# Softmax over rows: loads and stores of 8, 8 and seven times 16 rows, and broadcast multiplications on VectorE

## The chip, the cores and the metric

One core of a Trainium2 chip. The metric is the device time of one execution in microseconds (us), taken over several executions; all runs that are compared here are fast unless the text says otherwise. The profile is one of these executions. Its span, counted from the first load's issue to the last instruction, is about 2 us shorter than the device time.

## The reference

```python
x: (16, 1024, 512) float32
x_max = np.max(x, axis=-1, keepdims=True)
exp_x = np.exp(x - x_max)
return (exp_x / np.sum(exp_x, axis=-1, keepdims=True)).astype(np.float32)
```

That is 16384 rows of 512 numbers, 33.55 MB in and as much out.

## The kernel before

The rows are cut into chunks; a chunk of R rows per partition is one load. SBUF, the core's on-chip memory, is used in 128 partitions (the 128 in every shape below). The kernel keeps 96 rows per partition there, so the last two chunks go into rows that earlier ones have left. Within a chunk the work goes in groups of up to 8 rows per partition: VectorE takes the maxima (one instruction), ScalarE does exp and the sum row by row, VectorE the reciprocal, and GpSimd multiplies the group by it; for the last three groups VectorE multiplies. Loads are issued from SyncE, stores from ScalarE. Emission order is maximum and exponentials of group g, then scaling and store of group g-1.

```python
CHUNKS = [   # rows per partition, first row in SBUF
    (3, 0), (5, 3), (8, 8), (16, 16), (16, 32), (16, 48), (16, 64), (16, 80), (16, 0), (16, 16),
]
EARLY = 8                          # loads issued at once
AFTER_STORE = {2: [8], 3: [9]}     # chunk 8 is loaded after the store of chunk 2, 9 after 3
FINISH_BEFORE = (1, 2, 3)          # scale the waiting group before these chunks start
STORE_ROWS = {3: 8, 4: 8, 5: 8}    # chunks 3, 4, 5 are stored in halves of 8 rows
ON_VECTOR = 3
...
    def scale(g):
        k, a, b, since = groups[g]
        recip = stats.tile([P, b - a], F32, name="recip", tag="recip")
        nc.vector.reciprocal(out=recip, in_=sums[g])
        on_pool = g < len(groups) - ON_VECTOR
        if on_pool:
            nc.gpsimd.tensor_tensor(
                out=place[k][:, a:b, :], in0=place[k][:, a:b, :],
                in1=recip.unsqueeze(2).to_broadcast([P, b - a, d]),
                op=mybir.AluOpType.mult,
            )
        for r in () if on_pool else range(a, b):
            nc.vector.tensor_scalar_mul(
                out=place[k][:, r, :], in0=place[k][:, r, :],
                scalar1=recip[:, r - a : r - a + 1],
            )
        if since is not None:
            nc.scalar.dma_start(out=dst[k][:, since:b, :], in_=place[k][:, since:b, :])
        if b == CHUNKS[k][0]:
            for later in AFTER_STORE.get(k, ()):
                load(later)

        # in the order of the program
        for g, (k, a, _, _) in enumerate(groups):
            if waiting is not None and a == 0 and k in FINISH_BEFORE:
                scale(waiting)
                waiting = None
            rowmax(g)
            exps(g)
            if waiting is not None:
                scale(waiting)
            waiting = g
        scale(waiting)
```

(In this excerpt some lines are joined and comments are added.)

## Time and profile before

161.5 us. The DMA engines are full from the first microsecond to the last; the compute engines are about half busy.

| | before |
|---|---|
| device time, median of 6 | 161.51 us |
| span of the profile | 159.6 us |
| busy: VectorE, ScalarE, GpSimd | 82.6, 92.9, 91.2 us |
| DMA queues' share of 16 engines: loads, stores | 49.6%, 49.0% |
| last load landed | 109.1 us |
| last store issued | 134.0 us |
| first and last data packet | 1.0 us, 158.6 us |

### The profile page before, as it was taken

Reading aid. Unit: us, or ns where it says so; the run is one execution under the profiler, and the core shown is the slowest. Engines: PE = TensorE matmul, PEld = TensorE weight load, DVE = VectorE, ACT = ScalarE, POOL = GpSimd, SP = SyncE. Lnnn points to the kernel's source line nnn. Section 1 sums busy time; section 2 is a strip of 40 time slices with the busy share of each in tenths; the row PEclk is TensorE's granted clock in tenths of the full one; section 3 lists DMA queues with packets and bytes.
Section 4 is the critical chain, followed back from the end, with each engine's and each line's share of the span. In section 5 each row is a group of like instructions: output and inputs, shape, how many; then the busy total and the mean of one; then the engine's idle time right before and its main releaser. Section 6 shows DMA issues by size and latency. Waiting matters only on the chain.

```text
span 159.6 us, 442 instructions
## 1 busy us (share of the span) xinstructions
DVE 82.6 (52%) x58; ACT 92.9 (58%) x257; POOL 91.2 (57%) x18
## 2 busy tenths in 40 slices
DVE  0470903980966567393856768386479935000000
ACT  0719076039949796976979957993995760000000
POOL 0060912950899999999999999999930000000000
DMA  7999999999999999999999999989999999999994
GB/s 271 439 464 398 431 391 435 458 408 421 431 423 431 427 415 443 411 468 423 431 456 411 437 423 431 464 378 448 406 468 443 445 411 419 476 411 419 468 419 172
DMA packets 3315, 67.13 MB, mean 421 GB/s; under 512 B 368, under 2 KB 368, under 8 KB 624
## 3 DMA queue, kind: packets, MB, share of 16 engines
q1 hardware_dynamic: 1440, 33.56, 49.6%
q10 hardware_dynamic: 1872, 33.56, 49.0%
q14 instruction: 3, 0.02, 0.0%
HBM read 33.55 MB, written 33.55 MB: 420 GB/s over the span
## 4 chain that ended last, share of the span: by engine, by line
POOL 51%; issue 12%; ACT 11%; DVE 7%; DMA 3%; ACTq 0%; DVEq 0%; POOLq 0%
POOL held L150 51%; ACT held L135 11%; DVE held L157 4%; DMA held<-in_x_dram 3%; DVE shift L127 3%; ACTq L163 0%; DVE recip L147 0%; DVEq L209 0%; POOLq L150 0%; DVEq L147 0%; ACTq L135 0%
## 5 line engine op out<-in xcount | busy, mean ns | idle before, releaser
L135 ACT ACTIVATE held<-held,shift 128x512 f32<-128x512 f32 x128 | 90.4, 708 | 33.0 <-POOL held L150 29.9
L150 POOL TENSOR_TENSOR held<-held,recip 128x4096 f32<-128x4096 f32 (+2 forms) x14 | 91.0, 6529 | 25.8 <-DVE recip L147 25.8
L127 DVE TENSOR_REDUCE shift<-held 128x8 f32<-128x4096 f32 (+2 forms) x17 | 70.3, 4139 | 5.4 <-DMA held<-in_x_dram 5.4
L147 DVE RECIPROCAL recip<-sums 128x8 f32<-128x8 f32 (+2 forms) x17 | 3.4, 200 | 45.9 <-ACT held L135 45.9
L135 ACT ACTIVATION_READ_ACCUMULATOR held<-held,shift 128x1 f32 x128 | 24.0, 187 | 0.0
L157 DVE TENSOR_SCALAR held<-held,recip 128x512 f32<-128x512 f32 x24 | 10.0, 491 | 0.1
L135 ACT ACT_TABLE_LOAD x1 | 1.3, 1283 | 4.5 <-DMA held<-in_x_dram 4.5
L198 POOL MEMSET const-float32-0.0<- 128x1 f32 x1 | 0.1, 98 | 0.2 <-issue 0.2
L198 POOL MEMSET const-bfloat16-1.0<- 128x1 bf16 x1 | 0.1, 101 | 0.0
L198 POOL MEMSET const-uint8-127<- 128x1 uint8 x1 | 0.1, 101 | 0.0
L198 POOL MEMSET const-float32-1.0<- 128x1 f32 x1 | 0.1, 98 | 0.0
## 6 DMA issues: line engine op xcount, KB each, us to landing
held<-in_x_dram SPq DMA_DIRECT2D x7, 4096.0 KB, 39.1
out_dram<-held ACTq DMA_DIRECT2D x4, 4096.0 KB, 29.1
out_dram<-held ACTq DMA_DIRECT2D x7, 2048.0 KB, 37.9
held<-in_x_dram SPq DMA_DIRECT2D x1, 2048.0 KB, 11.5
held<-in_x_dram SPq DMA_DIRECT2D x1, 1280.0 KB, 7.1
out_dram<-held ACTq DMA_DIRECT2D x1, 1280.0 KB, 20.5
held<-in_x_dram SPq DMA_DIRECT2D x1, 768.0 KB, 4.4
out_dram<-held ACTq DMA_DIRECT2D x1, 768.0 KB, 15.8
```

The lines of the kernel that those rows point to most:

```text
L127: nc.vector.reduce_max(out=shift[g], in_=place[k][:, a:b, :], axis=AX, negate=True)
L135: nc.scalar.activation(out=place[k][:, r, :], in_=place[k][:, r, :], func=EXP, bias=shift[g][:, r - a : r - a + 1], scale=1.0, accum_out=s ...
L147: nc.vector.reciprocal(out=recip, in_=sums[g])
L150: nc.gpsimd.tensor_tensor(out=place[k][:, a:b, :], in0=place[k][:, a:b, :], in1=recip.unsqueeze(2).to_broadcast([P, b - a, d]), op=mybir.A ...
L157: nc.vector.tensor_scalar_mul(out=place[k][:, r, :], in0=place[k][:, r, :], scalar1=recip[:, r - a : r - a + 1],)
L198: nc = _bacc.Bacc("TRN2", target_bir_lowering=False, num_devices=1)
```

## The change

Its intent: fewer and larger transfers, and one instruction in place of eight for a scaling on VectorE. The diff, cut to its core (the old scaling is shown in the kernel above):

```diff
 CHUNKS = [
-    (3, 0), (5, 3), (8, 8), (16, 16), (16, 32), (16, 48), (16, 64), (16, 80), (16, 0), (16, 16),
+    (8, 0), (8, 8), (16, 16), (16, 32), (16, 48), (16, 64), (16, 80), (16, 0), (16, 16),
 ]
-EARLY = 8
-AFTER_STORE = {2: [8], 3: [9]}
+EARLY = 7
+AFTER_STORE = {1: [7], 2: [8]}
-FINISH_BEFORE = (1, 2, 3)
-STORE_ROWS = {3: 8, 4: 8, 5: 8}
+FINISH_BEFORE = ()
+STORE_ROWS = {}
@@ scale(g)
-        on_pool = g < len(groups) - ON_VECTOR
-        if on_pool:
-            nc.gpsimd.tensor_tensor(... broadcast of recip ...)
-        for r in () if on_pool else range(a, b):
-            nc.vector.tensor_scalar_mul(... row r ...)
+        engine = nc.gpsimd if g < len(groups) - ON_VECTOR else nc.vector
+        engine.tensor_tensor(
+            out=place[k][:, a:b, :],
+            in0=place[k][:, a:b, :],
+            in1=recip.unsqueeze(2).to_broadcast([P, b - a, d]),
+            op=mybir.AluOpType.mult,
+        )
```

More of the change, by code (lines that the diff above doesn't have):

```diff
@@ L147, in scale @@
         nc.vector.reciprocal(out=recip, in_=sums[g])
-        on_pool = g < len(groups) - ON_VECTOR
-        if on_pool:
-            nc.gpsimd.tensor_tensor(
-                out=place[k][:, a:b, :],
-                in0=place[k][:, a:b, :],
-                in1=recip.unsqueeze(2).to_broadcast([P, b - a, d]),
-                op=mybir.AluOpType.mult,
-            )
-        for r in () if on_pool else range(a, b):
-            nc.vector.tensor_scalar_mul(
-                out=place[k][:, r, :],
-                in0=place[k][:, r, :],
-                scalar1=recip[:, r - a : r - a + 1],
-            )
+        engine = nc.gpsimd if g < len(groups) - ON_VECTOR else nc.vector
[5 more added lines that the diff above has]
+        )
         if since is not None:
```

## The prediction

> **What bounds the kernel now.** I read the page first. The engines are 52 to 58% busy, so none of them is the limit. The DMA row and the queues are:
>
> ```profile
> DMA  7999999999999999999999999989999999999994
> DMA packets 3315, 67.13 MB, mean 421 GB/s; under 512 B 368, under 2 KB 368, under 8 KB 624
> q1 hardware_dynamic: 1440, 33.56, 49.6%
> q10 hardware_dynamic: 1872, 33.56, 49.0%
> ```
>
> The two queues (q1 loads, q10 stores) fill 98.6% of the sixteen engines' time between them. Only the first slice (until the first data) and the last (the final landing) have gaps. So the kernel is as long as 67 MB of traffic plus about 2.3 us of start and end (1.4% of 159.6 us). The page's chain of work names POOL with 51%, but that chain ends with the last scaling on VectorE at 134 us, and the span ends at 159.6. I therefore looked at the last stretches:
>
> ```profile
> core 0: us, DVE busy (x) ACT busy (x) POOL busy (x), PEclk, DMA share, GB/s
> ...
> 100.00:120.00 20.00, 12.57 (x13) 17.44 (x51) 17.21 (x3) 1.00 1.00 431
> 120.00:140.00 20.00, 11.42 (x20) 7.79 (x22) 0.00 (x0) 1.00 1.02 440
> 140.00:160.00 20.00, 0.00 (x0) 0.00 (x0) 0.00 (x0) 1.00 0.87 374
> ```
>
> No engine works after 134 us, and the DMA engines are still full. The last store was issued at 134.0 us; the queue then still had 24.6 us of packets (they end at 158.6), of which the last store itself is 8 x 1.213 = 9.7 us. So the last computation could have come about 15 us later before it cost anything. That slack is what the change can spend.
>
> How the two queues share is the second thing to read. A packet here is one partition's run: 32 KB for a load of 16 rows, 16 KB for a store of 8. Each transfer gives each engine eight packets. In the stretch from 60 to 70 us:
>
> ```profile
> q1 hardware_dynamic: 108, 3.01, 69.8%
> q10 hardware_dynamic: 103, 1.43, 33.3%
> ```
>
> Equal packets, not equal bytes: the queues alternate one for one, so a 32 KB load packet is followed by one 16 KB store packet and loads get two thirds. The trace has 1.213 us for a 32 KB packet and 0.611 for a 16 KB one; 8 x (1.213 + 0.611) = 14.6 us per load, and the last six loads land at 36.8, 50.9, 65.5, 80.0, 94.6 and 109.1 us, 14.1 to 14.6 apart. The tail after the last landing, on VectorE, is:
>
> ```profile
> 109.21 4.42 DVE L127 TENSOR_REDUCE shift<-held 128x8 f32<-128x4096 f32 x1 [0.81 <-DMA held<-in_x_dram]
> ...
> 116.75 3.52 DVE L157 TENSOR_SCALAR held<-held,recip 128x512 f32<-128x512 f32 x8
> 120.19 4.41 DVE L127 TENSOR_REDUCE shift<-held 128x8 f32<-128x4096 f32 x1
> ...
> 124.74 3.25 DVE L157 TENSOR_SCALAR held<-held,recip 128x512 f32<-128x512 f32 x8
> 130.48 0.20 DVE L147 RECIPROCAL recip<-sums 128x8 f32<-128x8 f32 x1 [2.48 <-ACT held L135]
> 130.72 3.26 DVE L157 TENSOR_SCALAR held<-held,recip 128x512 f32<-128x512 f32 x8
> ```
>
> The maximum of the last group stands behind the scaling of an earlier group, so 24.9 us pass from the landing of the last load to the issue of the last store.
>
> [...]
>
> **The change, part by part.** The bytes stay the same. The first two loads (3 and 5 rows) become one of 8, and it lands when the second did, about 7.4 us; the next 8 rows again at 12.4.
>
> Stores become 16 rows in three places where they were two halves of 8, so their packets grow from 16 to 32 KB. Per byte this is 0.6065 against 0.611 us for 16 KB: the 48 packets of 16 KB per engine that merge into 24 of 32 KB save about 0.2 us. Five DMAs fewer (18 instead of 23) save their semaphore packets of 9 ns, nothing.
>
> The first store comes later. First maximum 7.4 to 11.8, eight exponentials and the accumulator 5.8, to 17.6, reciprocal and hand-over 0.3, GpSimd 7.0: the first store is issued at 24.9 instead of 11.5 us. DMA stays busy meanwhile, with loads. In the trace the first store packet ran 3.7 us after the issue (11.5 to 15.2), because load packets lay ahead; so the first now runs at about 28.5.
>
> The sharing changes most. The third load (16 rows) lands at 12.4 + 8 x 1.27 = 22.6 (load packets with nothing beside them took 1.27 to 1.28 early on). At 28.5 five packets of the fourth are done. Left are 3 + 5 x 8 = 43 load packets on each engine, and each is paired with a store packet: 16 of 16 KB (the first two stores), then 27 of 32 KB. The last load therefore ends after 43 x 1.213 + 16 x 0.611 + 27 x 1.213 = 94.7 us, plus some 0.5 for the slower early ones: 123.7, landing at 124.1 instead of 109.1. This needs the store queue never to run dry: stores are issued, by the chain of 7.0 us scalings, at about 25, 34, 48, 62, 77 and 96 us, and needed at 28.5, 43, 58, 77, 97 and 116. It holds. The buffers for the last two loads come free at 58 and 78, before their turn.
>
> The tail from that landing, in the order in which the changed program puts VectorE's work: maximum 4.4, reciprocal and hand-over 0.4, tensor multiplication of the group before 4.4, maximum 4.4, exponentials 5.8 (the second multiplication, 4.4, lies beside them), reciprocal 0.3, multiplication 4.4: 24.1 us. The broadcast multiplications cost about 0.9 to 1.2 us each more than eight scalar ones (4.42 against 3.25 to 3.5); two of the three lie on this path. GpSimd's last scaling ends near 123, before VectorE's first at 129[...]. The last store is issued at 124.1 + 24.1 = 148.2 instead of 134.0.
>
> What is left for DMA at 123.7: 72 store packets less 43, that is 29, of which 21 lie before the last store: 21 x 1.213 = 25.5, to 149.2. An issue to an idle queue showed its first packet after 1.0 us (the first load), so the last store begins at about 149.3 to 149.7. The 15 us of slack is spent almost exactly; a gap of 0 to 0.5 us may open. Then 9.7 us of packets, the skew between engines included in the 25.5 only in part (up to 0.5), and 1.0 from last packet to end as before (158.6 to 159.6): span 160.0 to 160.9. The measured time was 1.9 above the span (161.45 against 159.6), which gives 161.9 to 162.8. I choose 162.1, since the larger packets give back 0.2.
>
> **The rivals.** First: pure traffic. If the loads end some us earlier, the last store still finds work before it, and the time is 161.2 to 161.6. For it speaks that 98.6% of the span is traffic that does not change; against it, that the pairing puts the last landing 15 us later. Second: the tail becomes the bound. Each us by which the last load lands later than 124, or by which the tail is longer than 24, then adds a whole us. If the broadcast multiplication ran at half the assumed rate on VectorE (8.8 us), the path would be 8.8 us longer and the time near 170. For that speaks only that no broadcast on VectorE is in this trace; on GpSimd the same form has no odd cost between widths (2.75 us for 1536, 7.02 for 4096 elements). Third: the late first store lets GpSimd be the bound. It starts at 17.9 instead of 8.7, but 13 equal scalings of 7.0 are 91 us, to 109 without waits and some 123 with waits for the slower loads; stores stay ahead of DMA throughout, so it costs nothing. Fourth: faster, by fewer and larger transfers. At most the 2.3 us of start and end plus 0.3 of packets could go, 1.6%, and the start is latency that stays.
>
> **Range and chances.** The two bounds, traffic at 161.3 and the tail at about 162.3, lie within 1 us of each other, and the time is the later. Errors of 1 to 2 us in the landing push it up and none pushes it below the traffic, so the range is lopsided: 161.2 to 163.5. Faster than 2% would need 158.3, below the traffic: 0.01. Slower than 2% is 164.7, a tail 2.5 us later than worked out: 0.06.
>
> **What the profile would show.** Right: equal packet counts and now about equal bytes of the two queues in the middle; the last load landing near 124; the last store issued near 148; VectorE's three multiplications of 4.4 us; DMA share near full to the end, with at most a small dent near 149. Wrong: stores not getting half of the bytes, a last landing before 120 (then 161.4) or after 127 (then 164 or more), multiplications on VectorE well off 4.4 us, or a hole in the DMA row in the middle, which would mean that the store queue ran dry.

The sum stands with all its terms: 124.1 for the last landing, 24.1 of tail, so the last store's issue at 148.2; that store's packets from 149.3 to 149.7 on, a span of 160.0 to 160.9, and with 1.9 outside it 161.9 to 162.8, of which the author chose 162.1. The terms of 4.4 us for a multiplication of 128x4096 by a broadcast on VectorE stand in it without their derivation, and the 4.42 set against the scalar ones had not been measured then. In the trace of the kernel before, the maximum over the same 128x4096 took 4.39 us in the mean, and eight multiplications by a scalar 3.25 to 3.52; the changed kernel's broadcast multiplications then took 4.42 to 4.43.

## The result, and the profile after

162.18 us, median of 6 runs (161.95 to 162.24), against 161.51 (161.40 to 161.61). The ratio is 1.0039, 95% interval 1.0026 to 1.0052. Ratios here are the mean time of one kernel's fast runs over that of the other's of the same rounds, so they are not quite the ratio of the medians. That is the same within 2%, and slower by 0.7 us beyond the noise.

The page of the changed kernel, DMA row and queues:

```profile
DMA  7999999899999999999999999999999999999996
...
q1 hardware_dynamic: 1296, 33.56, 49.6%
q10 hardware_dynamic: 1296, 33.56, 48.7%
```

Now both queues have 1296 packets, and DMA is still full, but for a dent near 149 us that the slices above are too coarse to show. In the middle, from 80 to 100 us (each line: queue, packets, MB, share of the 16 engines), the changed kernel has

```profile
q1 hardware_dynamic: 156, 4.59, 53.2%
q10 hardware_dynamic: 145, 4.23, 49.0%
```

where the kernel before had

```profile
q1 hardware_dynamic: 196, 5.90, 68.4%
q10 hardware_dynamic: 199, 2.74, 32.0%
```

In both, the two queues have packets in near equal number (196 to 199 before, 156 to 145 now), but the stores' packets have doubled in size (from 16 to 32 KB), so loads fall from 5.90 to 4.59 MB in the same 20 us. The loads are slowed by the stores (e6 below shows it with the stores alone changed), and the last one lands late. The tail in order of time (start, duration, engine and operation, and in brackets the idle time before it and what ended it):

```profile
124.00 4.42 DVE L127 TENSOR_REDUCE shift<-held 128x8 f32<-128x4096 f32 x1 [8.87 <-DMA held<-in_x_dram]
...
128.57 4.42 DVE L149 TENSOR_TENSOR held<-held,recip 128x4096 f32<-128x4096 f32 x1
...
132.91 4.41 DVE L127 TENSOR_REDUCE shift<-held 128x8 f32<-128x4096 f32 x1
...
137.47 4.43 DVE L149 TENSOR_TENSOR held<-held,recip 128x4096 f32<-128x4096 f32 x1
...
143.21 0.20 DVE L147 RECIPROCAL recip<-sums 128x8 f32<-128x8 f32 x1 [1.32 <-ACT held L135]
143.44 4.42 DVE L149 TENSOR_TENSOR held<-held,recip 128x4096 f32<-128x4096 f32 x1
147.96 0.34 ACTq L156 DMA_DIRECT2D out_dram<-held  x1
```

The last load is there at 124.0 (before: 109.1), and the last store is issued at 147.96 (before: 134.0). By stretches near that point:

```profile
core 0: us, DVE busy (x) ACT busy (x) POOL busy (x), PEclk, DMA share, GB/s
140.00:147.50 7.50, 6.15 (x3) 3.11 (x10) 0.00 (x0) 1.00 0.99 428
147.50:150.00 2.50, 0.37 (x1) 0.00 (x0) 0.00 (x0) 1.00 0.55 236
```

The kernel before has 433 GB/s in the same 2.5 us. So the queue did run dry for a moment: summed over the trace's packets, each engine idles 0.64 us on average in this stretch. The trace also shows why this costs less than 0.64: the sixteen engines end the packets of the second-last store between 147.9 and 149.2 us, and the last store's first packets run from 148.8. The engines that were early wait; the slowest one (149.2) does not, and its 149.2 plus 9.7 us for its eight packets of the last store gives 158.9, which is where the last packet ended (158.86). Before, the last packets of the engines ended 1.07 us apart; now, after the common restart, 0.3 apart.

The head is the other place with a difference. The first stretches of the kernel before, and then of the changed one:

```profile
0.00:2.00 2.00, 0.00 (x0) 0.00 (x0) 0.20 (x4) 1.00 0.48 135
2.00:4.00 2.00, 0.00 (x0) 0.00 (x0) 0.00 (x0) 1.00 0.99 407
```

```profile
0.00:2.00 2.00, 0.00 (x0) 0.00 (x0) 0.20 (x4) 1.00 0.73 131
2.00:4.00 2.00, 0.00 (x0) 0.00 (x0) 0.00 (x0) 1.00 0.87 336
```

From 2 to 4 us the changed kernel moves 336 GB/s against 407. The first packet of each engine took 1.00 to 2.23 us for 16 KB, where later ones take 0.61; before, 0.23 to 0.64 us for 6 KB, where later ones take 0.234. The first 16 rows had landed at 13.0 instead of 12.4 us.

So two theories stand for the 0.7 us. The **tail theory**: the last store comes too late. The **head theory**: the first loads start slower. The experiments undo one or the other.

### The profile page after: what moved, and what is told of

It is laid out like the page before. It is cut to its first block, busy times and chain, and to the rows that moved or that the text cites. A ratio compares the mean times of both kernels' runs of the same rounds, so it can differ in the third digit from the quotient of the medians.

```text
span 160.0 us, 405 instructions
## 1 busy us (share of the span) xinstructions
DVE 85.8 (54%) x35; ACT 92.9 (58%) x257; POOL 91.1 (57%) x17
## 3 DMA queue, kind: packets, MB, share of 16 engines
q1 hardware_dynamic: 1296, 33.56, 49.6%
q10 hardware_dynamic: 1296, 33.56, 48.7%
## 4 chain that ended last, share of the span: by engine, by line
DMA 52%; POOL 17%; issue 11%; DVE 9%; ACT 4%; DVEq 0%; POOLq 0%; SPq 0%
DMA held<-in_x_dram 33%; DMA out_dram<-held 20%; POOL held L149 17%; DVE held L149 6%; ACT held L135 4%; DVE shift L127 3%; DVE recip L147 0%; POOLq L149 0%; SPq L122 0%; DVEq L147 0%; DVEq L149 0%; DVEq L127 0%
## 5 line engine op out<-in xcount | busy, mean ns | idle before, releaser
L149 POOL TENSOR_TENSOR held<-held,recip 128x4096 f32<-128x4096 f32 x13 | 90.9, 7018 | 31.9 <-DVE recip L147 31.9
L127 DVE TENSOR_REDUCE shift<-held 128x8 f32<-128x4096 f32 x16 | 70.4, 4400 | 49.8 <-DMA held<-in_x_dram 49.8
L149 DVE TENSOR_TENSOR held<-held,recip 128x4096 f32<-128x4096 f32 x3 | 13.3, 4425 | 0.1
L147 DVE RECIPROCAL recip<-sums 128x8 f32<-128x8 f32 x16 | 3.2, 199 | 12.2 <-ACT held L135 12.2
```

The costliest lines, as they stand in the source:

```text
L127: nc.vector.reduce_max(out=shift[g], in_=place[k][:, a:b, :], axis=AX, negate=True)
L149: engine.tensor_tensor(out=place[k][:, a:b, :], in0=place[k][:, a:b, :], in1=recip.unsqueeze(2).to_broadcast([P, b - a, d]), op=mybir.AluO ...
```

## The experiments

Eleven kernels were run, and all gave correct results. "Outside" is device time less span, mean over the fast runs.

| run | time, us (median) | ratio to before, 95% interval | mean span | outside |
|---|---|---|---|---|
| changed kernel | 162.18 | 1.0039 (1.0026 to 1.0052) | 160.2 | 1.97 |
| e1 changed, small first loads | 162.32 | 1.0050 (1.0037 to 1.0062) | 160.1 | 2.23 |
| e2 changed, half stores | 162.26 | 1.0044 (1.0031 to 1.0056) | 160.2 | 2.04 |
| e3 changed, scalar multiplications | 161.86 | 1.0018 (1.0005 to 1.0032) | 160.1 | 1.83 |
| e6 before, whole stores only | 161.74 | 1.0016 (1.0004 to 1.0029) | 160.0 | 1.81 |
| e4 changed, 4.4 us more tail | 166.23 | 1.0295 (1.0281 to 1.0308) | 164.2 | 2.07 |
| e5 before, 4.4 us more tail | 161.59 | 1.0008 (0.9995 to 1.0021) | 159.8 | 1.84 |
| e7 changed, 16 rows first | 169.4 (its two fast runs; 171.1 with the two slow ones) | none | 167.5 | 1.89 |
| e8 before, 1 row first | 162.06 | 1.0042 (1.0027 to 1.0057) | 160.3 | 1.81 |
| e9 changed, padded program | 161.86 | 1.0028 (1.0014 to 1.0041) | 160.2 | 1.81 |
| e10 before, broadcasts only | 161.67 | 1.0018 (1.0002 to 1.0034) | 159.8 | 2.01 |
| e11 before, first loads only | 161.98 | 1.0030 (1.0017 to 1.0043) | 160.2 | 1.83 |

The kernel before, run beside them, had medians of 161.47 to 161.54 us, spans of 159.5 to 159.8 and 1.77 to 1.88 us outside.

### Is the slack of the tail spent? e4 and e5

The same edit in both kernels, one more multiplication (by ones) before the last store (the tile of ones and its filling are left out here):

```diff
+        if g == len(groups) - 1:
+            nc.vector.tensor_tensor(
+                out=place[k][:, a:b, :], in0=place[k][:, a:b, :],
+                in1=ones.unsqueeze(2).to_broadcast([P, b - a, d]),
+                op=mybir.AluOpType.mult,
+            )
         if since is not None:
```

> The changed kernel with one more multiplication of 128x4096 (by ones, the result is unchanged) on VectorE just before the last store: 4.4 us of extra tail. If the slack is nearly spent, as predicted (the last store is issued at 147.96 and the slowest engine has packets to 149.2, so about 0.4 us is left): a hole of 4 to 5 us in the DMA row and 166.0 to 166.6 us. If the tail does not bound the changed kernel and there is still slack: under 163 us.

> The kernel before with the same extra multiplication of 4.4 us before the last store. There the last store has some 15 us of other packets before it: 161.4 to 161.8 us, no hole. If the tail is on the path of the kernel before, as its chain of work says: 166 us.

166.23 us and 161.59. Of 4.4 us of added tail the changed kernel pays 4.05 (166.23 less 162.18) and the kernel before 0.1 (less 161.47, its neighbours' median). The stretches of the changed kernel with the longer tail:

```profile
147.50:150.00 2.50, 2.47 (x2) 0.00 (x0) 0.00 (x0) 1.00 0.06 26
150.00:152.50 2.50, 2.35 (x1) 0.00 (x0) 0.00 (x0) 1.00 0.00 0
```

and of the kernel before with it:

```profile
147.50:150.00 2.50, 0.00 (x0) 0.00 (x0) 0.00 (x0) 1.00 1.03 446
```

This is the clearest result: the changed kernel has about 0.4 us of slack left (4.43 less 4.05), the kernel before at least the 4.4 us that were added. Its whole slack is worked out, not tested: 148.9 (its slowest engine takes up the last store) less 134.0 is 14.9 us, or some 14 if the 0.84 us from the issue to the first packet (147.96 to 148.80 in the changed kernel) is counted. It also shows that the chain of work on the page of the kernel before, which ran through the tail, did not name what bounded it.

### Does the tail or the head cost the 0.7 us? e1, e2, e3, e6

e1, on the changed kernel:

```diff
-    (8, 0), (8, 8), (16, 16), ...
+    (3, 0), (5, 3), (8, 8), (16, 16), ...
-EARLY = 7
-AFTER_STORE = {1: [7], 2: [8]}
-FINISH_BEFORE = ()
+EARLY = 8
+AFTER_STORE = {2: [8], 3: [9]}
+FINISH_BEFORE = (1, 2, 3)
```

> The changed kernel with the kernel before's first loads (3, 5 and 8 rows instead of 8 and 8); whole stores and broadcast multiplications stay. The first 16 rows should land at 12.4 us again instead of 13.0. Head theory (the loss of the change lies in the slow first load alone): 161.5 us. Tail theory (the last store's issue is the bound, with almost no slack): stores start 14 us earlier, so 53 instead of 43 load packets per engine are paired with store packets; the last load lands near 125.8 instead of 124.0, and with 24 us of tail the last store is issued near 149.8: 163.2 to 163.8 us.

162.32 us: neither number. The first 16 rows landed at 12.4 as expected, but the last load landed at 124.0, not 125.8, and the last store was issued at 147.98; the pairing argument had overlooked that the store queue is empty for some 4 us before the first whole store (the last 16 KB store packets end at 53.9 us, the first of 32 KB start at 58.1), and loads run unpaired meanwhile: up to the end of the loads each engine took 50.8 store packets, not 53. DMA idles 0.86 us on average per engine from 147.5 to 150, and the span is 160.1.

e2, on the changed kernel:

```diff
-STORE_ROWS = {}
+STORE_ROWS = {2: 8, 3: 8, 4: 8}
```

> The changed kernel with chunks 2, 3 and 4 stored in halves of 8 rows, as before. Loads get two thirds of the bytes again, the last one lands near 108, and the last store is issued some 14 us before the queue is empty. Head theory: 162.1 to 162.4 us, the loss stays (smaller packets may add 0.2). Tail theory: the loss goes, 161.5 us.

162.26 us, as the head theory has it. The last load lands at 108.0, the last store is issued at 135.6, and the hole is gone (first the maximum that waits for the last load, then the stretch that held the hole):

```profile
108.03 4.42 DVE L127 TENSOR_REDUCE shift<-held 128x8 f32<-128x4096 f32 x1 [0.47 <-DMA held<-in_x_dram]
...
147.50:150.00 2.50, 0.00 (x0) 0.00 (x0) 0.00 (x0) 1.00 0.97 419
```

The loss stays. So taking away the hole alone doesn't bring the time back; and e1 shows that taking away the new head alone doesn't either.

e3, on the changed kernel (the diff of `scale` reversed):

```diff
-        engine = nc.gpsimd if g < len(groups) - ON_VECTOR else nc.vector
-        engine.tensor_tensor(... broadcast of recip ...)
+        ... GpSimd as before; on VectorE eight tensor_scalar_mul, as before
```

> The changed kernel with VectorE's three multiplications as eight by a scalar each, as before. The last landing stays at 124.0 and the last store is issued about 2 us earlier, near 146. Head theory: 162.1 us. Tail theory: 161.5 to 161.8 us.

161.86 us (161.67 to 162.19): between the two, 0.24 under the head theory's number and 0.06 over the tail theory's range. The store was issued at 145.8, with no hole. The spans (mean 160.1) are those of the changed kernel within noise; what fell is the time outside the span, from 1.97 to 1.83. That was not in either theory.

e6, on the kernel before:

```diff
-STORE_ROWS = {3: 8, 4: 8, 5: 8}
+STORE_ROWS = {}
```

> The kernel before with the halved stores merged into 16 rows and nothing else changed. The last load should land near 125.8 instead of 109.1, and the last store be issued near 147.7, the scalar multiplications keeping the tail at 22 us. Both theories, where the tail has a slack of about 2 us: 161.3 to 161.6 us; the difference from the small-head run is then VectorE's multiplications alone. If whole stores cost something by themselves (other than by the tail), it shows here as over 162.

161.74 us, 0.2 slower than before, a little above the range for "no cost" and below the 162 that was to show a cost of its own. The last load lands at 124.0 here too, and the last store is issued at 145.6: the whole stores alone move the last landing by 15 us, and no hole opens as long as the tail is short. e1 differs from e6 in VectorE's multiplications alone: 0.58 us, of which 0.42 is outside the span (2.23 against 1.81). Inside it, the hole of 0.86 us costs about 0.1.

### The first packet: e11, e7, e8

e11 is the head alone, on the kernel before:

```diff
-    (3, 0), (5, 3), (8, 8), (16, 16), ...
+    (8, 0), (8, 8), (16, 16), ...
-EARLY = 8
-AFTER_STORE = {2: [8], 3: [9]}
-FINISH_BEFORE = (1, 2, 3)
-STORE_ROWS = {3: 8, 4: 8, 5: 8}
+EARLY = 7
+AFTER_STORE = {1: [7], 2: [8]}
+FINISH_BEFORE = ()
+STORE_ROWS = {2: 8, 3: 8, 4: 8}
```

> The kernel before with the first two loads (3 and 5 rows) made one of 8, halved stores and scalar multiplications kept. Head theory: the first 16 rows land at 12.8 to 13.0 instead of 12.4, the span grows to 160.0 to 160.3, and the time is 161.85 to 162.1 us. If the first loads do not matter: 161.4 to 161.6.

161.98 us and spans of 160.0 to 160.3: 0.44 us over the kernel before, two thirds of what the whole change costs. In the profiled run, the fastest of the five, the first 16 rows landed at 12.6, and the first packets again took 0.69 to 1.61 us for 16 KB.

The slow first packets aren't the whole of it. Counted over the trace's packets, e11 had moved fewer bytes than the kernel before, by 0.45 us' worth (at 432 GB/s) at 14 us, but only by 0.08 at 20 us and by 0.10 to 0.11 from 60 us on: most of the slow start was won back, at the time when the kernel before begins with its first stores (15.2 us; in e11 28.8). The rest of the 0.40 us of span lies at the end: the slowest engine ends 0.88 us after the mean of the sixteen (before 0.73), and the span ends 1.18 us after the last packet (before 1.04). So "the head" is here the first loads with all that follows from them.

e7 and e8 were to show whether the size of the first packet is the cause. e7, on the changed kernel:

```diff
-    (8, 0), (8, 8), (16, 16), (16, 32), (16, 48), (16, 64), (16, 80), (16, 0), (16, 16),
+    (16, 0), (16, 16), (16, 32), (16, 48), (16, 64), (8, 80), (8, 88), (16, 0), (16, 16),
-AFTER_STORE = {1: [7], 2: [8]}
+AFTER_STORE = {0: [7], 1: [8]}
```

> The changed kernel with loads of 16, 16, 16, 16, 16, 8, 8, 16, 16 rows: the first packets are of 32 KB, and the stores are of 16 rows from the first on. Pairing: the first store starts near 41.5 us; the 40 load packets left on each engine are paired with 40 store packets of 32 KB; the last load lands near 129.7, the last store is issued near 153.7, the DMA row has a hole of about 5 us, 167 us (166 to 168). First-packet theory: the first 16 rows land at 13.3 to 14 us, later than with 16 KB packets (13.0) and with 6 KB (12.4); if it is not the packet's size, at 12.4 to 13.0.

e8, on the kernel before:

```diff
-    (3, 0), (5, 3), (8, 8), ...
+    (1, 0), (2, 1), (5, 3), (8, 8), ...
-EARLY = 8
-AFTER_STORE = {2: [8], 3: [9]}
-FINISH_BEFORE = (1, 2, 3)
-STORE_ROWS = {3: 8, 4: 8, 5: 8}
-AT_HEAD = {mybir.EngineType.SP: 3}
+EARLY = 9
+AFTER_STORE = {3: [9], 4: [10]}
+FINISH_BEFORE = (1, 2, 3, 4)
+STORE_ROWS = {4: 8, 5: 8, 6: 8}
+AT_HEAD = {mybir.EngineType.SP: 4}
```

> The kernel before with the first load of 3 rows split into 1 and 2. First-packet theory: first packets of 2 KB, the first 16 rows land at 12.0 to 12.3 us instead of 12.4, and the time is 161.2 to 161.6 us; the tail keeps its slack. If more and smaller transfers cost more than the first packet saves: 161.7 or more.

Both miss. The first maximum of e7, which waits for its first 16 rows:

```profile
12.23 4.42 DVE L127 TENSOR_REDUCE shift<-held 128x8 f32<-128x4096 f32 x1 [12.23 <-DMA held<-in_x_dram]
```

12.2 us, not 13.3 to 14, although each first packet of 32 KB took 1.5 to 2.25 us instead of 1.21. And e8, with first packets of 2 KB at their ordinary 0.08 to 0.2 us, had its first 16 rows only at 14.1: later packets were slow instead, and one engine fell 1.6 us behind the first. (This profile is of the slowest of its six runs, 162.59; but the fastest, 161.77, is over all runs of the kernel before too.) The landing of the first 16 rows against the number of loads that bring them is 12.2 (one), 12.6 to 13.0 (two of 8), 12.4 (three), 14.1 (four). There is no order by size in this, so "a larger first packet costs more in the end" is not supported. What remains is that the first packets are slow with 8 rows (0.69 to 2.23 us for 16 KB in the profiles of e11 and the changed kernel, where later ones take 0.61) and that this head alone costs 0.44 us.

e7's time (169.88 and 168.90 in its fast runs; the other two were slow) is above the 166 to 168 expected: the last load landed at 132.0, not 129.7, with the engines up to 4.4 us apart. From there the arithmetic of the tail holds: 24.0 us to the store's issue at 156.03, the first packet at 156.9, the last one's end at 166.8.

### The time outside the span: e9 and e10

The table shows 1.81 to 1.84 us outside the span for every kernel with scalar multiplications, and 1.89 to 2.23 with broadcasts. The trace has a third 8 KB fetch of instructions, at 120 to 139 us in the former. In e1, e2 and e4 it comes at 161.7, 161.9 and 166.1, after the span's end; in the changed kernel and e7 none is recorded. The broadcast makes VectorE's program 21 instructions shorter.

e9, on the changed kernel (the tile `spare`, which nothing reads, is left out here):

```diff
+            if g == 4:
+                for _ in range(21):
+                    nc.vector.memset(spare, 0.0)
             rowmax(g)
             exps(g)
```

> The changed kernel with 21 tiny VectorE instructions (128x8 memsets of a tile that nothing reads) put in before the fifth group, so that VectorE's program is about as long as that of the kernel before. In the runs so far the time outside the span is 1.80 to 1.87 us where VectorE's scalings are eight scalar instructions, and 1.91 to 2.27 where they are one broadcast; in the first kind the trace has a third 8 KB instruction fetch between 120 and 140 us, in some of the second kind it comes only after the end of the span. Fetch theory: the third fetch falls inside the span, the time outside it goes to 1.80 to 1.87, and the total to about 162.0. If the length of the program has nothing to do with it: 1.95 or more outside the span, 162.1 to 162.2 in all.

e10, on the kernel before (the diff of `scale` alone):

```diff
-        ... on VectorE eight tensor_scalar_mul
+        engine = nc.gpsimd if g < len(groups) - ON_VECTOR else nc.vector
+        engine.tensor_tensor(... broadcast of recip ...)
```

> The kernel before with VectorE's 24 scalar multiplications replaced by three broadcast ones, nothing else. The tail gets about 3 us longer and has 15 us of slack: the span stays at 159.6 to 159.8. Fetch theory: 1.95 to 2.25 us outside the span, 161.65 to 162.0 in all. If the fetch theory is wrong: 161.4 to 161.6.

Both came out as the fetch theory has it. The queue of instruction fetches on the page of e10, which has two within its span (the third is at 161.7):

```profile
q14 instruction: 2, 0.02, 0.0%
```

and of e9, where padding brought the third back, at 128.8 us:

```profile
q14 instruction: 3, 0.02, 0.0%
```

e9 has 1.81 us outside its span, as the kernel before has, and 161.86 in all (161.71 to 162.42; its spans scatter more, 159.9 to 160.6). e10 has 2.01 and 161.67. Its profiled run, 162.57, was the one outlier of six. So the length of VectorE's program, and not the broadcast as such, makes the difference. Whether the late fetch itself costs the time is not shown apart from that, nor why it is 0.42 us in e1 against e6 and 0.13 to 0.21 elsewhere.

### All eight combinations

Taken together, the runs hold every combination of the change's three parts (the new head with its order of scaling, whole stores, broadcasts). Median us, and in brackets the mean span:

| | half stores, scalar | half stores, broadcast | whole stores, scalar | whole stores, broadcast |
|---|---|---|---|---|
| first loads 3, 5, 8 | before: 161.51 (159.7) | e10: 161.67 (159.8) | e6: 161.74 (160.0) | e1: 162.32 (160.1) |
| first loads 8, 8 | e11: 161.98 (160.2) | e2: 162.26 (160.2) | e3: 161.86 (160.1) | changed: 162.18 (160.2) |

The head costs 0.4 to 0.6 us with half stores, but 0.1 and -0.1 with whole ones; whole stores cost 0.2 and 0.65 with the old head, and about -0.1 with the new one. So the two don't add up: by the ratios to the kernel before, both together cost 0.5 us (give or take 0.3, an estimate from the table's intervals) less than the sum of each alone. For the kernels with broadcasts the traces say why the head doesn't matter there: the last store's first packet runs at 148.8 in e1 as in the changed kernel, because in both the last load lands at 124.0 and the same tail follows. Here the tail is the bound; without the hole (e2) the last packet ends no sooner, at 158.89 us against 158.86. For the scalar ones the reason is open.

No experiment beat the kernel before.

## Why the prediction was right

The time was within 0.1 us of 162.1. The pairing and the tail were right; that the sum came so close was luck in part, for small errors at its start and end didn't enter or nearly cancelled.

**Traffic bounds both kernels: held.** DMA is full throughout in both (the two queues fill 98.6% of the sixteen engines' span before, 98.3% after), but for the hole in the changed one.

**The pairing of packets and the last landing: held.** 156 load packets to 145 store packets from 80 to 100 us, and the landing at 124.0 against 124.1 predicted. The kernel with whole stores alone (e6) moved the landing by the same 15 us, and half stores (e2) moved it back to 108.0.

**The tail: held.** 24.0 us from landing to issue against 24.1, multiplications of 4.42 to 4.43 us where the sum had 4.4, the issue at 147.96 against 148.2, the packets of the second-last store to 149.2. e4 shows that 0.4 us of slack is left. Of the 15 us, e5 tested 4.4, and e6 moved the issue by 11.6 us without a hole. GpSimd's last scaling had ended, at 123.2 us, before VectorE's first multiplication began, at 128.6, as said. Where the two met, the multiplication took longer: in e10 VectorE's first one starts 0.46 us before GpSimd's last one ends, and took 4.75 us; the other two took 4.42.

**The first loads: failed.** The prediction had the 8-row load land "when the second did, about 7.4 us; the next 8 rows again at 12.4". They landed at 8.1 and 13.0, and on the kernel before the head alone costs 0.44 us (e11), which the prediction didn't have. That didn't spoil its sum: the last load still landed at 124.0, and the changed kernel with the old head (e1) is no faster, 162.32. The prediction had "the start is latency that stays": the first packet does start 1.0 us after the issue in both kernels, but that ignored how the first transfer is cut.

**What the hole costs: over-booked.** The prediction let the end follow the last store's issue one for one. The hole was larger than its 0 to 0.5 (0.64 us mean per engine) and cost only about 0.1, because the early engines wait and the slowest sets the end. It had the last store's packets run from 149.3 to 149.7 for 9.7 us, to 159.0 to 159.4; they ran from 148.8 to 158.86. Against that 0.1 to 0.5 us too much stand 0.17 too little for the time from the last packet to the end of the span (1.0 taken over, 1.17 measured) and 0.07 in the next term; they nearly cancelled.

**The time from span to device time: 1.9 assumed, 1.97 measured, 1.82 before.** The prediction did not see that this grows with the shorter program that the broadcasts make: by 0.18 us in e10, and not at all once the program is padded (e9).

The parts alone cost 0.44 (head), 0.13 (broadcasts) and 0.20 (whole stores) by the medians. That their sum, 0.77, is near the 0.67 of the whole doesn't show that they add: the table of combinations shows that they don't, and by the ratios the sum is 1.0 against 0.63.

**Open** stays why the head and the whole stores cost what they do. The first packet's size alone doesn't explain it (e7, e8). The traces show where some of it lies. The time from the last packet to the end of the span, which the prediction took over as 1.0, differs with the layout of the transfers and repeats within it: 1.04 to 1.07 us in the kernel before, e5 and e10, 1.27 and 1.28 in e1 and e6, 1.18 to 1.21 in e11 and e2, 1.17 in the changed kernel, e3, e4 and e9. In e6 that is nearly all: its last packet ends at 158.60 (before 158.58) although its packets take 0.25 us less per engine, and 0.24 of its 0.25 us of longer span come after it. What takes longer there isn't shown.

## What to carry to other kernels

Where DMA bounds a kernel, ask of each change first what it does to the slack between the last computation and the moment at which the queue would run dry; here the change ate some fourteen microseconds of it (the last store's issue went from 134.0 to 147.96 us) for 0.7 us in all, and the next 4.43 us were then paid nearly in full (4.05 in e4). Where two queues have packets in near equal number, as here (196 to 199, then 156 to 145), look at their packet sizes: the bytes went with them (5.90 to 2.74 MB, then 4.59 to 4.23), so enlarging the stores slowed the loads. And when a predicted sum comes out right, test its terms, in combination too: here some were wrong in opposite directions, and what the parts cost alone is not what they cost together.
